# Feed-forward blocks in groups of four, by seven block products in place of eight, with weight sums formed by adding transfers

## Chip, cores and metric

The kernel runs on one NeuronCore of a Trainium2 chip. The metric is the device time of one execution in microseconds (us): here the median of three runs. All tensors are float32.

## What is computed

One inference step of a backbone of two layers. Each layer has a mixer part (attention, pooling, projections) and a feed-forward part (FFN). There are 640 tokens, 128 of context and 512 latent ones, and the model is 1024 wide. The change touches only the FFN and what lies around it:

```
def conv_ffn(h, w_up, conv_w, conv_b, w_down):
    u = h @ w_up
    g, val = u[..., :D_FF], u[..., D_FF:]
    gp = jnp.pad(g, ((0, 0), (1, 1), (0, 0)))
    g = gp[:, :-2] * conv_w[0] + gp[:, 1:-1] * conv_w[1] + gp[:, 2:] * conv_w[2] + conv_b
    return (jax.nn.silu(g) * val) @ w_down
```

`D_FF` is 2816, so `w_up` is 1024 x 5632 and `w_down` 2816 x 1024. The layer then adds the result to the residual `x`, with a gain that the modulation (adaLN) gives.

## The kernel before

Features lie on the 128 partitions and tokens on the free axis. So the normed input of the FFN is 8 tiles (`KT` = 8) of 128 features x 640 tokens, and a half of the tokens (`HT`) is 320 columns. The 2816 inner features are 22 blocks (`NF`) of 128.

**A product.** A float32 matmul is done as three products of reduced parts. `split` makes a high part by a copy on ScalarE (ACT, L251) and a low part by a subtraction on VectorE (DVE, L252). `dense` (L270) then multiplies high by high, high by low, and low by high. One block of weights (128 output features, 1024 inputs) by 640 tokens takes 8 x 3 x 2 = 48 matmuls of 128 x 320, which accumulate in one PSUM tile `mm`.

**Weights.** `load` brings a block of 512 KB by a transfer on SyncE's queue (SP) into one of three `ws` buffers, and `weights` splits it in two operations of 1024 columns into `wh` and `wl` (two buffers each).

**The FFN.** `ffn` goes through the 22 blocks in chunks of 9, 8 and 5 (`CHUNKS`). For a block f it computes the gate block (column block f of `w_up`) and then the value block (column block 22 + f). ScalarE copies the gate into `gp`, VectorE does the convolution (L1148, L1150, L1151), ScalarE a tanh (L1152), VectorE the rest of the silu (L1153, L1154) and the product with the value block (L1159). The result is split into two `u` tiles, which stay in SBUF (20 buffers). At a chunk's end eight output blocks of `w_down` are computed from these `u` tiles, and `residual` (L580) adds each to `x`. The last chunk goes through `project`, which does all output blocks for the first half of the tokens and then for the second, so that the norm's sums can follow.

**Order.** The order of a Tile program is that of its generators. In the first layer, `along` spreads the modulation's products (`ada`: 56 loads of 512 KB, matmuls marked L524) among those of the FFN. The Tile scheduler may move instructions of an engine within its dependencies.

## Time and profile before

| | |
|---|---|
| median of three runs (lowest, highest) | 2315.22 us (2312.96 to 2317.17) |
| span of the profiled execution | 2318.4 us |
| TensorE busy | 2256.9 us (97%) |
| VectorE busy | 1246.9 us (54%) |
| ScalarE busy | 830.5 us (36%) |
| POOL (GpSimd) busy | 150.9 us (7%) |
| DMA, mean over the span | 97 GB/s |

The profiled execution is one more run, and its own time is its span: 3.2 us over the median. A busy share is an average over stages with different limits. What a change in one stage is worth has to be read from that stage: from the chain of waits there and from the windows' busy times.

### The profile page before, as it was taken

The numbers are of one execution on the slowest core, as the hardware profiler recorded it, in microseconds if no ns is written. First come the engines' busy times: TensorE is split into PE (matmuls) and PEld (weight loads), VectorE is DVE, ScalarE is ACT, GpSimd is POOL, SyncE is SP. The second block draws the span as 40 slices with busy tenths as digits, with TensorE's granted clock in tenths as the row PEclk, the third lists the DMA queues.
The fourth block names the chain that finished last, engine by engine and source line by source line (L and its number), as shares of the span: only waits on it lengthen the run. The fifth ranks groups of instructions, "written<-read, shape, count | busy, mean of one in ns | idle before, by whom it ended". The sixth has DMA issues, their size and how long they took to land.

```text
span 2318.4 us, 38736 instructions
## 1 busy us (share of the span) xinstructions
PE 2256.9 (97%) x15863; PEld 2118.1 (91%) x15863; DVE 1246.9 (54%) x2262; ACT 830.5 (36%) x1578; POOL 150.9 (7%) x365
## 2 busy tenths in 40 slices
PE   7999999999999999999999999999999999999998
PEld 4898999998988888999988989999998999999997
DVE  5676736652555432543577767376535654354353
ACT  4466325541423211221334663255423332132132
POOL 1122001210000000000001220021100000000000
PEclk8999999999999999999999999999999999999999
DMA  8242343126505665322142423321124022222221
GB/s 306 69 104 53 99 117 92 46 57 194 177 12 182 189 181 172 98 78 73 55 127 69 104 52 98 82 57 52 46 80 149 23 78 82 73 73 74 74 66 62
DMA packets 283249, 224.69 MB, mean 97 GB/s; under 512 B 12223, under 2 KB 256694, under 8 KB 283072
## 3 DMA queue, kind: packets, MB, share of 16 engines
q1 hardware_dynamic: 282400, 221.43, 33.4%
q8 instruction: 125, 2.05, 0.4%
q0 software_dynamic: 672, 0.79, 0.1%
q14 instruction: 52, 0.43, 0.1%
HBM read 195.54 MB, written 8.29 MB: 88 GB/s over the span
## 4 chain that ended last, share of the span: by engine, by line
PE 81%; DVE 6%; ACT 4%; DMA 3%; issue 2%; POOL 0%; DVEq 0%; ACTq 0%
PE mm L270 50%; PE mm L287 8%; PE d L270 8%; PE o L728 3%; PE pt L637 3%; PE sm L524 2%; PE s L270 1%; DMA ws<-in_w_out 1%; ACT wh L251 1%; PE sm L335 1%; PE s L1012 1%; PE s L1013 1%; PE s L1014 1%; PE s L832 1%; DVE wl L252 1%
## 5 line engine op out<-in xcount | busy, mean ns | idle before, releaser
L252 DVE TENSOR_TENSOR wl<-ws,wh 128x1024 fp32r<-128x1024 f32 (+3 forms) x276 | 277.2, 1009 | 483.5 <-ACT wh L251 469.4
L251 ACT ACTIVATE wh<-ws 128x1024 fp32r<-128x1024 f32 (+3 forms) x276 | 242.8, 886 | 801.6 <-PE mm L270 556.0
L270 PE MATMUL mm<-hh,wh 128*128 128x320 f32 (+1 forms) x2016 | 466.6, 312 | 4.5 <-ACT wh L251 1.5
L270 PE MATMUL mm<-hh,wl 128*128 128x320 f32 (+1 forms) x2016 | 462.0, 310 | 0.8 <-DVE wl L252 0.7
L270 PE MATMUL mm<-hl,wh 128*128 128x320 f32 (+1 forms) x2016 | 461.1, 310 | 0.0
L270 PEld LDWEIGHTS mm<-hh,wh 128*128 128x128 f32 (+1 forms) x2016 | 333.8, 187 | 28.5 <-issue 21.5
L270 PEld LDWEIGHTS mm<-hh,wl 128*128 128x128 f32 (+1 forms) x2016 | 335.4, 187 | 4.6 <-DVE wl L252 1.9
L270 PEld LDWEIGHTS mm<-hl,wh 128*128 128x128 f32 (+1 forms) x2016 | 335.5, 187 | 2.2 <-issue 1.0
L270 PE MATMUL mm<-u,wh 128*128 128x320 f32 x1024 | 193.1, 310 | 0.0
L270 PEld LDWEIGHTS mm<-u,wh 128*128 128x128 f32 x1024 | 160.1, 188 | 6.2 <-issue 6.2
L626 POOL TENSOR_SCALAR p<-p,st 128x640 f32<-128x640 f32 (+1 forms) x160 | 117.8, 737 | 612.6 <-DVE st L625 556.9
L642 DVE TENSOR_TENSOR ptl<-pt,pth 128x512 fp32r<-128x512 f32 (+1 forms) x208 | 118.4, 584 | 46.2 <-PE o L728 23.2
L624 ACT ACTIVATE p<-s,st 128x640 f32<-128x640 f32 (+1 forms) x160 | 113.4, 709 | 67.0 <-DVE st L623 61.5
L641 ACT ACTIVATE pth<-pt 128x512 fp32r<-128x512 f32 (+1 forms) x208 | 103.8, 514 | 66.5 <-PE pt L637 64.7
L623 DVE TENSOR_REDUCE st<-s 128x1 f32<-128x640 f32 (+1 forms) x160 | 113.8, 711 | 21.7 <-PE s L1014 9.2
L580 DVE SCALAR_TENSOR_TENSOR x<-mm,g2h,x 128x128 f32<-128x128 f32 (+2 forms) x144 | 55.9, 434 | 128.2 <-PE mm L270 99.3
L287 PE MATMUL mm<-hh,wr 128*128 128x320 f32 x512 | 118.3, 313 | 3.2 <-ACT hh L251 3.2
L270 PE MATMUL d<-hh,wh 128*128 128x320 f32 x352 | 118.4, 336 | 2.3 <-ACT wh L251 0.5
L270 PE MATMUL mm<-u,wl 128*128 128x320 f32 x512 | 116.5, 308 | 0.0
L637 PE MATMUL pt<-ident,p 128*128 128x128 f32 x672 | 110.1, 276 | 5.7 <-DVE ptl L642 4.4
L270 PE MATMUL d<-hh,wl 128*128 128x320 f32 x352 | 109.5, 311 | 0.0
L270 PE MATMUL d<-hl,wh 128*128 128x320 f32 x352 | 109.3, 310 | 0.0
(312 smaller groups left out, 3954.2 us busy)
## 6 DMA issues: line engine op xcount, KB each, us to landing
wa<-in_w_ada SPq DMA_DIRECT2D x96, 512.0 KB, 3.9
ws<-in_w_up SPq DMA_DIRECT2D x88, 512.0 KB, 3.9
ws<-in_w_in SPq DMA_DIRECT2D x74, 512.0 KB, 4.0
ws<-in_w_down SPq DMA_DIRECT2D x34, 512.0 KB, 4.2
ws<-in_w_out SPq DMA_DIRECT2D x16, 512.0 KB, 4.2
xd<-x SPq DMA_DIRECT2D x16, 320.0 KB, 4.5
x<-xd SPq DMA_DIRECT2D x16, 320.0 KB, 6.5
ws<-in_w_down SPq DMA_DIRECT2D x16, 320.0 KB, 3.2
```

The lines of the kernel that those rows point to most:

```text
L251: nc.scalar.activation(hi, src, AF.Copy)
L252: nc.vector.tensor_tensor(lo, src, hi.bitcast(F32), ALU.subtract)
L270: nc.tensor.matmul(dst, lhsT, r[:, HT * h:HT * h + HT], start=first, stop=last)
L287: nc.tensor.matmul(ps, lhsT, r[:, HT * h:HT * h + HT], start=first, stop=last)
L580: self.nc.vector.scalar_tensor_tensor(self.x[j][:, xs], ps[pi], gate[:, j, s:s + 1], self.x[j][:, xs], ALU.mult, ALU.add)
L623: nc.vector.tensor_reduce(st[:, 0:1], s, axis=AX.XY if len(s.shape) == 3 else AX.X, op=ALU.max, negate=True)
L624: nc.scalar.activation(self.half(p) if len(s.shape) == 3 else p, s, AF.Exp, bias=st[:, 0:1], accum_out=st[:, 1:2])
L626: nc.gpsimd.tensor_scalar(p, p, st[:, 2:3], 1.0, ALU.mult, ALU.mult)
L637: nc.tensor.transpose(pt[:, P * t:P * t + P], p, self.ident)
L641: nc.scalar.activation(hi, v, AF.Copy)
L642: nc.vector.tensor_tensor(lo, v, hi.bitcast(F32), ALU.subtract)
L728: nc.tensor.matmul(state["o"][:, 256 * u:256 * u + 256], vl[a](t + 1), hl[r][:, t, :], start=t == 0 and r == 0, stop=t == 4 and r == 1)
```

## The change

The first two gate and value blocks of a layer, and the last six blocks of the down product, stay as they were. All else is done in **jobs**, 28 in a layer. A job takes two weight blocks side by side, cuts their inputs in two halves and the tokens in two halves, and computes the 2 x 2 blocks of the result by seven block products (Winograd's form of Strassen's scheme) instead of eight. A block product is 12 matmuls (4 input tiles x 3 parts) of 128 x 320, called a slot here, so a job has 84 in place of 96. There are 20 up jobs (gates and values of two blocks each) and 8 down jobs (`CHUNKS` is 8, 8, 6 now).

The seven products need sums and differences:

- **Of weights.** Three of the seven weight operands are sums ("3", "2", "4"). They are formed by transfers that add to their target, on POOL's queue (`fast_sum`): one of 512 KB from `w` in DRAM into a `ws` tile that two plain loads filled before, and two of 256 KB from SBUF to SBUF in a `wb` tile.
- **Of activations.** VectorE forms four mixed blocks ("1" to "4") with `mix_b`, and both parts of each are kept in tiles `tq`. For the up jobs this is done once a layer. For the down jobs, `u` goes to DRAM (`ud`), comes back in groups of eight tiles `ul`, and is mixed and split when the columns change (`chunk`).
- **Of results.** ScalarE copies three of the products out of PSUM (tile `cp`), and VectorE adds.

Splits of weights come as seven of 512 columns a job in place of two of 1024 a block. The convolution's first step moves from VectorE to ScalarE. A job begins every seven slots, and neighbours overlap: `SLOTS` says where each product stands, and `PREP_AT` (in slots from the job's start) when its loads, sums and splits are issued. PSUM holds six banks `q` and two `sm` in this phase. ScalarE, VectorE, POOL and SP keep the program's order while jobs run (`Ordered`). `x` is put into DRAM ahead of the jobs and comes back ahead of the first down job. The last `project` loads and splits its weights a second time for the second half of the tokens, and the modulation's weights have two buffers `wa` of their own.

```diff
-CHUNKS = (9, 8, 5)
+PLAIN_F = 2
+CHUNKS = (8, 8, 6)
...
+        def call(*a, **k):
+            r = f(*a, **k)
+            if self.kern.ordered:
+                self.kern.tc.keep_in_program_order(r)
+            return r
...
+    def fast_load(self, job, what):
+        dma = self.nc.sync.dma_start
+        top, low = job["src"]()
...
+        if what == "sums":
+            dma(parts[:, 0], rows(top)[:, 0])
+            dma(parts[:, 1], rows(low)[:, 0])
...
+        elif what == "top":
+            dma(w.rearrange("p (k n) -> p k n", n=P), top)
...
+            self.flush()
+        else:
+            w = w[:, 0:512].rearrange("p (k n) -> p k n", n=P)
+            dma(w, rows(low)[:, 1])
+            job["a"]["22"] = w
...
+    def fast_sum(self, job, n):
+        a = job["a"]
+        d, x = {"3": (job.get("sums"), job["src"]()[1]), "2": (a.get("2"), a.get("1")), "4": (a.get("4"), a.get("2"))}[n]
+        self.nc.gpsimd.dma_start(d, x, accum_op=ALU.add)
...
+        for t, n, p in at:
+            job = jobs[n]
+            due((n, WSIDE[p]), (job["vn"], VSIDE[p]))
+            first, last = p in ("1", "2", "5"), p != "5"
+            if first:
+                job[bank[p]] = self.q()[:, :HT]
+            ps, w, v = job[bank[p]], job["w"][WSIDE[p]], job["v"][VSIDE[p]]
+            nk = v.shape[2]
+            for k in range(nk):
+                ks = slice(P * k, P * k + P)
+                for i, (x, y) in enumerate(((0, 0), (0, 1), (1, 0))):
+                    nc.tensor.matmul(
+                        ps, w[:, x, ks], v[:, y, k, :], start=first and k == 0 and i == 0,
+                        stop=k == nk - 1 and i == 2, skip_group_check=True)
+                step(t, k)
+                yield 408
+            done(job, p)
...
-                nc.vector.tensor_scalar(
-                    y, gp[:, 0:641], cw[:, 0, f:f + 1], self.conv_b[l][:, f:f + 1], ALU.mult, ALU.add)
...
+            lambda: nc.scalar.activation(
+                y, gp[:, 0:641], AF.Identity, bias=self.conv_b[l][:, f:f + 1], scale=cw[:, 0, f:f + 1]),
...
+            return [(None, lambda f=f: load(f)) for f in range(f0, f0 + 8)], {
+                "1": spl("11"), "2": spl("21"), "5": mix("1") + mix("3") + spl("1") + mix("2") + mix("4") + spl("2"),
+                "7": spl("3"), "4": spl("4"), "3": spl("22")}
...
+        for f0 in (0, 8):
+            loads, works = chunk(f0)
+            behind(jobs[-1], "1", loads)
+            for n in ("1", "2", "5", "7", "4", "3"):
+                behind(jobs[-1], n, works[n])
...
+SLOTS = {"1": 0, "2": 1, "6": 3, "5": 4, "7": 6, "4": 9, "3": 12}
+PREP_AT = {
+    "load": {"sums": -11, "top": -9, "22": -7}, "s3": -9.5, "s2": -5.5, "s4": -4.5,
+    "11": -6, "12": -5, "22": -4, "2": -0.75, "1": -0.25, "3": 0.75, "4": 3.5}
```

**Where instructions stand.** On TensorE, among the last up blocks of the second layer, the order before has three kinds of matmul a tile (`hh`, `hl` the input's parts, `wh`, `wl` the weights'), eight times over, and then the next tile:

```order
L270 MATMUL mm_3011_21267<-hh_66,wh_3009_21263 128x320 x2
L270 MATMUL mm_3011_21267<-hl_67,wh_3009_21263 128x320 x2
L270 MATMUL mm_3011_21267<-hh_66,wl_3010_21264 128x320 x2
L270 MATMUL mm_3019_21332<-hh_66,wh_3017_21328 128x320 x2
L270 MATMUL mm_3019_21332<-hl_67,wh_3017_21328 128x320 x2
L270 MATMUL mm_3019_21332<-hh_66,wl_3018_21329 128x320 x2
```

At that place it now has seven slots: parts of two neighbouring jobs in turn (`hq00`, `hq10`, `hq11` are blocks of the input, `tq` the mixed ones, `wh`, `wl`, `wp` and `hq01` the operands of the weights):

```order
L1363 MATMUL q_2969_19749<-tq_2928_19349,wl_2971_19764 128x320 x12
L1363 MATMUL q_2984_19851<-hq00_66,wh_2974_19773 128x320 x12
L1363 MATMUL q_2988_19871<-hq10_68,wl_2975_19791 128x320 x12
L1363 MATMUL q_2969_19749<-tq_2929_19350,hq01_67 128x320 x12
L1363 MATMUL q_2984_19851<-tq_2927_19348,wp_2981_19836 128x320 x12
L1363 MATMUL q_2998_19935<-tq_2926_19347,wh_2982_19845 128x320 x12
L1363 MATMUL q_2978_19811<-hq11_69,wp_2979_19815 128x320 x12
```

A tile `mm` was finished in one go; now a bank `q` gets 12 matmuls, is left, and gets 12 more some slots later.

On VectorE, where the second layer turns from up to down columns, each down block had one split of its weights and three pieces of the residual's addition:

```order
L252 TENSOR_TENSOR wl_2894_20023<-ws_2892_20020,wh_2893_20022 128x1024
L580 SCALAR_TENSOR_TENSOR x_2661_17996<-mm_2887_19898,g2h1_179,x_2661_17996 128x128
L580 SCALAR_TENSOR_TENSOR x_2661_17996<-mm_2887_19898,g2h1_179,x_2661_17996 128x192
L580 SCALAR_TENSOR_TENSOR x_2661_17996<-mm_2887_19898,g2h1_179,x_2661_17996 128x320
L252 TENSOR_TENSOR wl_2898_20087<-ws_2896_20084,wh_2897_20086 128x1024
L580 SCALAR_TENSOR_TENSOR x_2662_17997<-mm_2891_19962,g2h1_179,x_2662_17997 128x128
L580 SCALAR_TENSOR_TENSOR x_2662_17997<-mm_2891_19962,g2h1_179,x_2662_17997 128x192
```

In the changed order the first such turn (first layer) has the mixing of the loaded blocks `ul` and their splits into `tq`, among the splits of weights (`wp`) and the last blocks' convolution (`u2`, `gp`):

```order
L171 TENSOR_TENSOR ul_1620_10714<-ul_1621_10716,ul_1620_10714 128x320
L171 TENSOR_TENSOR ul_1622_10725<-ul_1623_10727,ul_1622_10725 128x320
L171 TENSOR_TENSOR ul_1627_10741<-ul_1628_10743,ul_1627_10741 128x320
L171 SCALAR_TENSOR_TENSOR u2_1631_10758<-u2_1631_10758,y_1632_10759 128x128
L171 TENSOR_TENSOR gp_1166_7302<-cp_1608_10628,q_1609_10630 128x320
L171 TENSOR_TENSOR ul_1629_10752<-ul_1630_10754,ul_1629_10752 128x320
L171 TENSOR_TENSOR tq_1162_7298<-ul_1620_10714,tq_1162_7298 128x320
L171 TENSOR_TENSOR wp_1640_10850<-wb_1610_10648,wp_1640_10850 128x512
L171 TENSOR_TENSOR tq_1162_7298<-ul_1622_10725,tq_1162_7298 128x320
L171 SCALAR_TENSOR_TENSOR u2_1631_10758<-u2_1631_10758,y_1632_10759 128x512
L171 TENSOR_TENSOR tq_1162_7298<-ul_1627_10741,tq_1162_7298 128x320
L171 TENSOR_TENSOR tq_1162_7298<-ul_1629_10752,tq_1162_7298 128x320
```

These rows are 12 of the 47 operations that stand there from the first split of the new block "11" to the last of the block "2".

On POOL, late in the second layer, stood only the clearing of the padding columns of `gp`, and then the last norm's diagonal matrices:

```order
L1141 MEMSET gp_3060_21916 128x1 x3
L1141 MEMSET gp_3074_22047 128x1 x3
L1141 MEMSET gp_3088_22178 128x1 x3
L1141 MEMSET gp_3102_22309 128x1 x3
L1141 MEMSET gp_3116_22440 128x1 x3
L1231 TENSOR_SCALAR gdiag_3175_22820<-ident_74,colsB_425 128x128 x4
```

Now the adding transfers of each job stand there in a row, with the semaphores that each waits for (DMAHW: loads on SP's queue; DMASW: transfers of POOL's own queue; DVE: a split that has read the target):

```order
L171 DMA ws_3084_20618<-in_w_up 128x8x128 [waits DMAHW7_49,DMAHW6_49]
L171 DMA wb_3088_20652<-ws_3084_20618 128x512 [waits DMASW7_49,DMAHW0_49,DMASW3_49,DVE_49]
L171 DMA wb_3088_20652<-wb_3088_20652 128x512 [waits DMASW0_49,DVE_49]
L171 DMA ws_3103_20755<-in_w_up 128x8x128 [waits DMAHW4_49,DMAHW3_49]
L171 DMA wb_3107_20789<-ws_3103_20755 128x512 [waits DMASW6_49,DMAHW5_49,DMASW2_49,DVE_49]
L171 DMA wb_3107_20789<-wb_3107_20789 128x512 [waits DMASW3_49,DVE_49]
```

The first transfer of a job waits for its two loads, the second for the first transfer among others, the third for the second.

## Rows read from the trace of the kernel before

**Rows 1.** Head of the page: span, busy time by engine, granted clock
```profile
span 2318.4 us, 38736 instructions
...
PE 2256.9 (97%) x15863; PEld 2118.1 (91%) x15863; DVE 1246.9 (54%) x2262; ACT 830.5 (36%) x1578; POOL 150.9 (7%) x365
...
PEclk8999999999999999999999999999999999999999
```

**Rows 2.** The page's chain that ended last, by engine (part 4)
```profile
PE 81%; DVE 6%; ACT 4%; DMA 3%; issue 2%; POOL 0%; DVEq 0%; ACTq 0%
```

**Rows 3.** Pieces of the chain: start us, us, engine, tile, line, count
```profile
716.71 3.71 PE mm L270 x24
...
720.99 4.59 PE mm L270 x30
...
933.33 216.68 PE mm L270 x1476
...
1846.66 401.54 PE mm L270 x2736
```

**Rows 4.** Windows: us, busy of PE, PEld, DVE, ACT, POOL; clock, DMA, GB/s
```profile
10.00:20.00 10.00, 9.04 (x56) 6.43 (x56) 5.01 (x19) 5.97 (x22) 5.02 (x10) 1.00 1.04 391
...
712.00:798.00 86.00, 86.00 (x643) 74.60 (x641) 43.12 (x62) 23.17 (x37) 1.06 (x18) 1.00 0.62 183
...
1846.00:2256.00 410.00, 409.26 (x2787) 408.73 (x2788) 191.61 (x263) 109.76 (x171) 3.38 (x60) 1.00 0.25 74
```

**Rows 5.** DVE's groups, 1846 to 2256 us: busy, mean ns, idle before
```profile
L252 DVE TENSOR_TENSOR wl<-ws,wh 128x1024 fp32r<-128x1024 f32 x57 | 69.8, 1224 | 145.6 <-ACT wh L251 145.1
...
L1150 DVE SCALAR_TENSOR_TENSOR y<-gp,colsD,y 128x641 f32<-128x641 f32 x22 | 19.4, 887 | 0.7
...
L252 DVE TENSOR_TENSOR w<-ws,w 128x512 fp32r<-128x512 f32 x2 | 1.3, 690 | 0.0
...
L1159 DVE TENSOR_TENSOR u<-u,mm 128x320 f32<-128x320 f32 x2 | 1.0, 484 | 0.1
...
L1154 DVE SCALAR_TENSOR_TENSOR u<-fth,y 128x512 f32<-128x512 f32 x22 | 15.1, 685 | 0.0
...
L1153 DVE SCALAR_TENSOR_TENSOR u<-fth,y 128x128 f32<-128x128 f32 x22 | 6.4, 291 | 16.2 <-ACT fth L1152 16.2
```

**Rows 6.** ACT's groups by form, the same stretch
```profile
L1152 ACT ACTIVATE fth<-y 128x641 f32<-128x641 f32 x22 | 16.3, 742 | 62.7 <-DVE y L1151 62.7
...
L1146 ACT ACTIVATE gp<-mm 128x320 f32<-128x320 f32 x22 | 9.7, 443 | 0.0
...
L251 ACT ACTIVATE w<-ws 128x512 fp32r<-128x512 f32 x2 | 1.1, 616 | 0.0
```

**Rows 7.** Timeline of DVE, two instructions of 1950.8 to 1956 us
```profile
1953.40 1.23 DVE L252 TENSOR_TENSOR wl<-ws,wh 128x1024 fp32r<-128x1024 f32 x1
1954.54 0.82 DVE L252 TENSOR_TENSOR u<-u,u 128x640 fp32r<-128x640 f32 x1
```

**Rows 8.** DMA issues: count, KB each, us to landing; one queue
```profile
q0 software_dynamic: 672, 0.79, 0.1%
...
ws<-in_w_up SPq DMA_DIRECT2D x88, 512.0 KB, 3.9
...
ws<-in_w_down SPq DMA_DIRECT2D x16, 320.0 KB, 3.2
...
cos<-in_k_cosm SPq DMA_DIRECT2D x2, 256.0 KB, 3.0
...
sel<-in_k_selb POOLq DMA_DIRECT2D x1, 448.0 KB, 6.9
...
itr<-in_cache_gqa_v SPq DMA_DIRECT2D x2, 64.0 KB, 1.8
```

**Rows 9.** Timeline of POOL at the start: start us, us
```profile
2.52 0.56 POOL L393 DMA_DIRECT2D sel<-in_k_selb  x1
...
4.08 0.50 POOL L410 DMA_DIRECT2D rows<-in_g_norm_ffn  x1
```

More of the change, by code (lines that the diff above doesn't have):

```diff
@@ L33 @@
 NF = DFF // P
-CHUNKS = (9, 8, 5)
+PLAIN_F = 2
+CHUNKS = (8, 8, 6)
+GW = 644
 WINDOWS = (2, 4, 8, 16)
@@ L123, in __getitem__, with __init__ @@
         return self.tiles[at[1]][:, at[2]]
+class Halves:
+    def __init__(self, parts):
+        self.parts = parts
+    def __getitem__(self, at):
+        rows, sl = at
+        h = sl.start // HT
+        return self.parts[h][rows, sl.start - HT * h:sl.stop - HT * h]
 class Feed:
@@ L1124, in out_proj @@
     def out_proj(self, l, m, after):
-        mh = [self.split(a, out=b) for a, b in zip(m, self.h)]
+        for a, (hi, lo) in zip(m, self.h):
+            for h in range(2):
+                sl = slice(HT * h, HT * h + HT)
+                self.split(a[:, sl], out=(hi[:, sl], lo[:, sl]))
+        mh = self.h
         put = lambda j: [self.ph.tile([P, D], F32R, tag="wr", bufs=16, name=self.nm("wr")) for _ in range(2)]
@@ new lines, in ffn, with shifted @@
+        v = {"11": self.hq[0][0], "21": self.hq[1][0], "22": self.hq[1][1], "1": tq[0], "2": tq[1], "3": tq[2],
+             "4": tq[3]}
+        spare = self.hq[0][1].rearrange("p v k n -> p (v k n)")
+        self.w22 = [spare[:, 1024 * a:1024 * a + 1024].rearrange("p (v n) -> p v n", v=2) for a in range(2)]
+        self.n22 = 0
+        us = {}
+        def shifted(h):
+            return [(xs, pi, slice(xs.start + 1 + s, xs.stop + 1 + s)) for s, xs, pi in self.pieces(h)]
+        gps = [self.g(643, name="gp") for _ in range(NGP)]
@@ new lines, in value_plain, with ev @@
+        def value_plain(f):
+            def ev(ps, h):
+                for hh in range(2) if h is None else (h,):
+                    a = self.half(us[f][:, :T], hh)
+                    nc.vector.tensor_tensor(a, a, ps[hh] if h is None else ps, ALU.mult)
+                if h != 0:
+                    out(f)
+            return ev
+        wpt = lambda: self.ph.tile([P, 1024], F32R, tag="wp", bufs=NWP, name=self.nm("wp"))
+        w0 = self.weights(wup(DFF), KT, P, out=(wpt(), wpt()))
+        ws = [self.weights(wup(0), KT, P), self.weights(wup(P), KT, P)]
@@ new lines, in behind @@
+        def behind(job, n, works):
+            after = job.setdefault("after", {})
+            after[n] = after.get(n, []) + works
+        for f0 in (0, 8):
[3 more added lines that the diff above has]
+                behind(jobs[-1], n, works[n])
+            for j in range(0, KT, 2):
+                jobs.append({
+                    "src": lambda f0=f0, j=j: down_src(f0, j), "v": v, "vn": f0, "mixed": True,
+                    "ev": Later(lambda j=j: down_job(j))})
+            if f0 == 0:
+                behind(jobs[-KT // 2], "1", [("x", self.unspill)])
@@ new lines, in ffn, with last_load, last_split @@
+        f0, nf = sum(CHUNKS[:2]), CHUNKS[2]
+        acts, ul = [], {}
+        def last_load(i):
+            self.flush()
+            ul[i] = self.g(name="ul")
+            nc.sync.dma_start(ul[i], ud[f0 + i])
+        def last_split(i, slot):
+            hi, lo = [Halves([slot[:, i % 2, 2 * w + h, :] for h in range(2)]) for w in range(2)]
+            for h in range(2):
+                hs = slice(HT * h, HT * h + HT)
+                self.split(ul[i][:, hs], out=(hi[:, hs], lo[:, hs]))
+            acts.append((hi, lo))
@@ new lines, in ffn @@
+        behind(jobs[-2], "6", [(None, lambda i=i: last_load(i)) for i in range(nf)])
+        for i, (product, name) in enumerate((("6", "2"), ("5", "1"), ("7", "3"))):
+            behind(jobs[-1], product, [(None, lambda n=n, name=name: last_split(n, v[name])) for n in (2 * i, 2 * i + 1)])
+        self.ordered = True
+        yield from self.fast(jobs)
+        self.ordered = False
+        src = lambda j: self.wsrc("w_down", l, P * f0, nf, P * j, P)
+        yield from self.project(src, nf, acts, self.g2h[l], after, None, stat)
```

386 lines of the change are left out of this document (307 added, 79 removed).

## Prediction

> **What bounds the kernel now.** I read the head of the page first. TensorE is busy for 2256.9 of 2318.4 us, VectorE for 1246.9 and ScalarE for 830.5, and the granted clock is at its upper level (2.4 GHz, shown as 9 or 1.00) in every slice but the first [rows 1, 4]. The chain that ended last runs through TensorE for 81% of the span [rows 2]. Within the two feed-forward layers the chain of waits shows more: it holds whole pieces of TensorE with no wait in them. One has 1476 matmuls of 320 columns in 216.68 us, another 2736 in 401.54 us [rows 3]. Both give 0.1468 us a matmul (216.68/1476, 401.54/2736). So in this stage a matmul less is 0.147 us less, as long as nothing else becomes late. The table of windows says how far the others are from that: in 1846 to 2256 us VectorE is busy for 191.6 of 410 us, ScalarE for 109.8, POOL for 3.4, and the DMA engines for 25% of their time [rows 4].
>
> **Matmuls removed (A).** The order has 12676 matmuls of 128x320 before and 12004 after; all others keep their number. That is 672 less: 28 jobs in each of 2 layers, 12 less in each. 672 x 0.1468 = **-98.6 us**. A job is now 84 x 0.1468 = 12.3 us of TensorE (14.1 before), one of its seven slots of 12 matmuls 1.76 us. Everything below is set against 12.3 us a job.
>
> **VectorE and ScalarE in a steady job.** On VectorE one operation starts about 0.09 us ahead of its forerunner's end (1.23 us shown, next start 1.14 later [rows 7]), so I take mean less 0.09: 0.60 for 512 columns, 0.40 for 320, 0.80 for 641 [rows 5]. A job on a gate block has 7 subtractions of 512 (4.2), two convolutions of 2 x 0.80 + 0.20 + 0.60 (4.8) and four or so additions of half blocks (1.3): 10.3 us. A value job has 4.2 + 7 x 0.40 = 7.0, a down job some 7.7. ScalarE in a gate job has 7 x 0.62 + 3 x 0.47 + 0.6 for the halves, and 4 x 0.74 for the convolutions' first steps and tanh [rows 6]: 9.3 us. All lie below 12.3 and beside it: **0**. The cover is thin for gate jobs alone, and a value job follows each.
>
> **The adding chain on POOL (G).** Three transfers of a job follow each other there, and the queue is in order: the 512 KB sum from DRAM (waits for its two loads), the first SBUF sum (waits for that one and for a split), the second (waits for the first); then the next job's. So a job's pace is at least the time to landing of the 512 KB sum, plus that of a 256 KB sum, plus an issue. No adding transfer is in the trace. Bounds: as plain transfers 3.9 us for 512 KB, 3.0 for 256 KB, 0.55 for an issue [rows 8, 9]: 7.5 us. With all doubled, 14.4 us, which is 2.0 over the job: 56 x 2.0 = +113. I take the middle: 64 KB land in 1.8 us and 512 KB in 3.9 [rows 8], so some 2 us do not grow with size, and only what does is doubled by reading the target too: 6.3 + 4.2 + 0.55 = 11.1 us, **0**, with 1.3 us a job to spare. The only row of a large transfer on POOL's queue, 448 KB in 6.9 us, was in the first microseconds, where the DMA share was at its full [rows 4, 8]; it is nearer to the middle than to either end.
>
> The Trainium skill ("DMA: Bandwidth & Descriptors", Anatomy of one DMA, SWDGE path) gives about 2.0 us and bytes over 436 GB/s: 3.2 and 2.6 us, a chain of 6.4 us as an estimate, and the sum would be the same. Of the additions it says nothing there; "Collectives: The Full Stack" says that a reducing transfer reads two sources and so runs at about half the rate of a copy. No row here shows that.
>
> **Chunk changes (B).** Twice in a layer the jobs turn from up to down columns, or to the next eight, and VectorE and ScalarE must then mix and split the eight `u` blocks anew. By the order, VectorE has 47 operations between the first split of the new "11" and the last of "2" at the first change (35 of 320 columns at 0.40, 5 of 512 and one of 512 with three operands at 0.60, 4 of 641 at 0.80, 2 of 128 at 0.21: 21.2 us), 44 at the second (18.4 us). The matmuls that want them come 9.75 slots after the slot in which the loads are issued: 17.2 us, less 3.2 for the first load of 320 KB [rows 8] = 14.0 us. TensorE waits 7.2 + 4.4 us a layer: **+23 us** for two. Low bound 10 (only the excess over the whole 17.2 us, 4.0 + 1.2 a layer), high bound 36 (the splits of other products go on the path too).
>
> **Start of the jobs (C).** The first job's sums can't be prepared long ahead. Load 3.9 + 6.3 + 4.2 + a split of 1.3 = 15.7 us, against two plain blocks of 96 matmuls' time (14.1 us) ahead of it: 1.6 us late in a layer. Its splits also stand behind the two convolutions of the plain blocks in the order, so I take 3 a layer, **+6**; 0 to 20 (nothing, or 10 a layer where the loads start only with the last plain block).
>
> **DMA where adaLN weights come along (D).** In layer 0 56 loads of 512 KB go beside the feed-forward. Behind each of them TensorE has 24 or 30 matmuls (25.5 in the mean), a cycle of 4.28 us for 24, which is 0.76 more than 24 x 0.1468 [rows 3]. A job of 84 takes 3.3 of them, so 56 loads last for 17 jobs of 12.3 + 3.3 x 0.76 = 14.8 us. The stretch with these loads had the DMA engines at 62% for 183 GB/s, the undisturbed one at 25% for 74 GB/s: about 295 GB/s at full share; the first microseconds moved 391 [rows 4]. By 295 a job's 1.7 MB of ada and 1.3 MB of plain loads take 0.39 and 0.30 of its time, the 512 KB sum 0.12 (0.25 if it counts double); by 391 the two others 0.09 (0.18) and `u` 0.06: 0.96 to 1.18 in all. At the low end nothing is lost, at the high one 17 x 14.8 x 0.18 = 45 us; I take a third or so, **+16**. In layer 1 the same sum without ada, over 12.3 us, is 0.70 to 0.94: 0.
>
> **Order as written (E).** Four engines now keep the program's order, so a late operation holds those behind it; the rows cannot show it. 0 to 20 us, **+6** (0.1 us a job). The last projection (F) loads and splits its weights twice: 18 matmuls, 2.6 us, against a split of 768 columns, about 0.9 on either engine [rows 5, 6]: 0.
>
> **Sum.** -98.6 + 23 + 6 + 16 + 6 = -47.6 on the profiled execution's 2318.4 gives 2270.8 us. That span is 3.2 us above the median of 2315.2, so against the median **2268 us**. Its own range, from the bounds of B to E (most of them cannot end alike): 2240 to 2297.
>
> **The rivals.**
> *Stalls absorbed (A alone, nearly).* B at its low bound, C, D and E near 0 to 4: 2315.2 - 98.6 + 13 = 2230 us. For it: TensorE's chain has hundreds of microseconds without a wait [rows 3], and over half of VectorE's time is idle [rows 4]. Against it: by the order VectorE gets some 680 operations more, in bursts at the chunk changes.
> *DMA full in layer 0.* Adds count double and contention is paid: D at 45: 2315.2 - 98.6 + 23 + 6 + 45 + 6 = 2297 us. For it: 62% before the change [rows 4]. Against it: in the first microseconds 391 GB/s were moved [rows 4].
> *The adding chain sets the pace (the other side).* POOL's order is strict, so if its three steps take c us, each job takes c. At 14.4 us: 2315.2 - 98.6 + 113 + 23 + 6 = 2359 us. From c = 13.6 on, the gain is gone (56 x 1.24 = 69.6 = 98.6 - 29). For it: the 448 KB row of 6.9 us [rows 8], and 1024 pieces of 512 bytes in a queue that has carried 672 packets in the whole run [rows 8]. Against it: issues on POOL take 0.50 to 0.56 us whatever they carry [rows 9].
> A rule of the Trainium skill speaks for this rival: by "SBUF - State Buffer", the "DVE blocks DMA" trap, VectorE operations with one input that use both of its ports keep GpSimd from writing descriptors (620 ns become some 3100). VectorE's operations among these jobs have two inputs each, which that page has disturbing GpSimd's reads alone, so I give it 0.02 of this rival's chance; no row here shows it. By its figures, as an estimate, each of three issues would come 2.5 us later and a job's chain would be 18.6 us.
>
> **How the numbers follow.** Chances: the forecast 0.46, stalls absorbed 0.18, DMA full 0.13, adding chain 0.23. The range: 2222 (below the absorbed case, 2216.6 being A without any loss) to 2340, which leaves out the upper half of the chain's case. 0.2% of the time, 4.6 us, is what a measurement here can tell from no change. Faster: 0.46 + 0.18 + 0.13, less 0.06 for their upper ends, and 0.03 for a chain just over the job's time: 0.74; the same 0.05; slower 0.21.
>
> **What the profile after would show.** Right: 14503 matmuls ordered, those of the jobs at 0.147 us, TensorE's pieces without a wait several jobs long, and gaps at two places a layer, ended by VectorE's `tq` splits. The adding transfers of 512 KB land in 5 to 7 us, those of 256 KB in 3.5 to 5. Wrong if each job ends on a wait for a weight sum (`wp`, `wh` split late, released by POOL's queue), if the sums land in more than 8 us, if a job of layer 1 takes much over 12.3 us, or if the granted clock falls to its lower level in the new gaps.

## Result and the profile after

The changed kernel takes 2441.92 us (2432.15 to 2450.62, four runs) against 2315.75 us before: 1.0539 times as long, 95% interval 1.0508 to 1.0569. The forecast was 2268 us, with a range of 2222 to 2340; it was wrong in sign and by 174 us.

The head of its page (span; busy time by engine; granted clock; the chain that ended last, by engine), beside [rows 1, 2]:

```profile
span 2437.1 us, 39673 instructions
...
PE 2225.1 (91%) x15191; PEld 2067.4 (85%) x15191; DVE 1491.6 (61%) x2974; ACT 1064.9 (44%) x2170; POOL 345.8 (14%) x425
...
PEclk8999999999998999998999999999999899998899
...
PE 37%; DMA 15%; DVE 8%; ACT 4%; issue 3%; SPq 1%; POOL 0%; DVEq 0%; ACTq 0%; POOLq 0%
```

The shares of the chain are not to be compared as they stand: it can be followed back only to 759 us here, and to 88 us before, so they add up to 68% and 96% of the span. Of what was followed, TensorE has 54% where it had 84%, and transfers 22% where they had 3%. In five slices besides the first, all where the jobs run, the granted clock is below its upper level.

The windows (columns as in [rows 4]) of 200 us of up jobs in the first layer, of 220 us of steady up jobs in the second, and of all jobs of the second layer:

```profile
780.00:980.00 200.00, 168.71 (x1166) 144.84 (x1164) 99.79 (x185) 72.41 (x136) 35.66 (x32) 0.93 0.97 242
1957.00:2177.00 220.00, 205.12 (x1317) 203.28 (x1318) 144.25 (x264) 106.16 (x209) 53.43 (x50) 0.95 0.93 192
1922.00:2365.00 443.00, 384.34 (x2397) 375.96 (x2398) 292.28 (x572) 201.51 (x413) 101.36 (x88) 0.92 0.90 189
```

The DMA engines are 90 to 97% busy, where they were 25% and, with the adaLN loads, 62% [rows 4]. They move 192 GB/s at a share of 0.93: some 206 GB/s at full share, against 295 before. So it is not bytes alone; the bytes are dearer. The DMA issues (count, KB each, us to landing) and the queue of the adding transfers say which:

```profile
q0 software_dynamic: 87328, 59.53, 18.2%
...
wa<-in_w_ada SPq DMA_DIRECT2D x96, 512.0 KB, 6.4
...
ws<-in_w_up SPq DMA_DIRECT2D x120, 256.0 KB, 5.7
...
ws<-in_w_up POOLq DMA_DIRECT2D x40, 512.0 KB, 7.9
wb<-ws POOLq DMA_DIRECT2D x56, 256.0 KB, 4.8
wb<-wb POOLq DMA_DIRECT2D x56, 256.0 KB, 4.4
```

The 512 KB sum from DRAM lands in 7.9 us (I took 6.3), the SBUF sums in 4.8 and 4.4 (I took 4.2). The plain loads have become slow too: a 512 KB `wa` load lands in 6.4 us in the median, where 512 KB took 3.9 [rows 8]. On POOL's timeline a pair of jobs looks like this (start us, us; in brackets the idle time ahead and its releaser):

```profile
2025.36 0.85 POOL L171 DMA_DIRECT2D wb<-wb  x1 [4.84 <-DMA wb<-ws]
2026.21 1.58 POOL L171 DMA_DIRECT2D ws<-in_w_up  x1
2033.26 0.89 POOL L171 DMA_DIRECT2D wb<-ws  x1 [5.46 <-DVE u L171]
2037.62 0.84 POOL L171 DMA_DIRECT2D wb<-wb  x1 [3.47 <-DMA wb<-ws]
2038.15 1.90 POOL L171 DMA_DIRECT2D ws<-in_w_up  x1
2047.82 0.88 POOL L171 DMA_DIRECT2D wb<-ws  x1 [7.76 <-DMA ws<-in_w_up]
```

From one DRAM sum (`ws<-in_w_up`) to the next it is 11.9 us, and from that to the one at 2054.32 another 16.2; over the 16 jobs from 1957.28 to 2176.87 the mean is 13.7. TensorE needs 12.3 a job. The waits of all engines, and those of TensorE (us in total, times, the longest):

```profile
ACT wp L171 <- DMA wb<-ws: 232.4, 47, 15.9
POOL wb L171 <- DMA wb<-ws: 223.4, 46, 10.7
```

```profile
PE q L1363 <- ACT cp L171: 56.3, 20, 9.1
PE sm L584 <- DMA wa<-in_w_ada: 44.3, 28, 5.0
PE q L1363 <- ACT wh L171: 39.4, 11, 5.1
```

ScalarE waits for an SBUF sum 47 times. Behind that split of `wp` stand, in the written order, the splits of `wh` and the copies `cp`, and these are what TensorE waits for, with the adaLN loads.

From the first matmul of the jobs to the last it takes, in us (28 jobs a layer need 28 x 12.33 = 345 of TensorE alone, and in the first layer 56 x 0.76 = 43 more for adaLN, 388):

| run | median us | before, beside it | ratio, 95% interval | jobs, layer 0 | jobs, layer 1 |
|---|---|---|---|---|---|
| changed kernel | 2441.9 | 2315.8 | 1.0508 to 1.0569 | 495.5 | 443.1 |
| no_sums | 2297.2 | 2318.7 | 0.9877 to 0.9921 | 415.4 | 377.0 |
| plain_copies | 2355.5 | 2318.7 | 1.0143 to 1.0192 | 462.8 | 391.8 |
| early_dram_sum | 2450.6 | 2318.7 | 1.0552 to 1.0586 | 497.3 | 444.3 |
| sums_dve | 2329.4 | 2318.7 | 1.0039 to 1.0069 | 427.6 | 393.3 |
| only_dram_sum | 2334.4 | 2315.3 | 1.0053 to 1.0110 | 434.4 | 387.2 |
| only_sbuf_sums | 2336.6 | 2315.3 | 1.0075 to 1.0105 | 441.2 | 391.8 |
| no_sums_no_turns | 2263.6 | 2315.3 | 0.9760 to 0.9793 | 402.0 | 360.8 |
| sums_pool | 2375.2 | 2315.3 | 1.0244 to 1.0281 | 457.2 | 419.6 |
| dve_early | 2331.8 | 2317.3 | 1.0044 to 1.0080 | 430.4 | 396.6 |
| dve3_dma1_early | 2333.0 | 2317.3 | 1.0045 to 1.0084 | 436.1 | 394.0 |
| dve2_dma2_early | 2351.6 | 2317.3 | 1.0122 to 1.0167 | 449.8 | 394.0 |
| no_top_loads | 2385.4 | 2317.4 | 1.0275 to 1.0310 | 463.8 | 420.4 |
| no_turns_free | 2241.8 | 2317.4 | 0.9659 to 0.9691 | 393.8 | 356.4 |
| dve_dma_at_turns | 2335.7 | 2317.4 | 1.0063 to 1.0093 | 434.0 | 396.9 |
| dve_dma_at_start | 2348.7 | 2317.4 | 1.0124 to 1.0154 | 441.6 | 403.3 |
| sums_dve_free | 2289.2 | 2316.8 | 0.9859 to 0.9889 | 411.7 | 379.6 |
| after_free | 2557.0 | 2316.8 | 1.1010 to 1.1051 | 556.3 | 505.0 |
| dve3_dma1_free | 2284.9 | 2316.8 | 0.9838 to 0.9878 | 413.4 | 376.4 |

### The profile page after: what moved, and what is told of

The parts are those of the page before. It is cut to its first block, busy times and chain, and to the rows that moved or that the text cites. A ratio compares the mean times of both kernels' runs of the same rounds, so it can differ in the third digit from the quotient of the medians.

```text
span 2437.1 us, 39673 instructions
## 1 busy us (share of the span) xinstructions
PE 2225.1 (91%) x15191; PEld 2067.4 (85%) x15191; DVE 1491.6 (61%) x2974; ACT 1064.9 (44%) x2170; POOL 345.8 (14%) x425
## 3 DMA queue, kind: packets, MB, share of 16 engines
q0 software_dynamic: 87328, 59.53, 18.2%
## 4 chain that ended last, share of the span: by engine, by line
PE 37%; DMA 15%; DVE 8%; ACT 4%; issue 3%; SPq 1%; POOL 0%; DVEq 0%; ACTq 0%; POOLq 0%
PE q L1363 11%; PE mm L324 7%; DMA wb<-ws 5%; DMA wa<-in_w_ada 4%; PE q L341 4%; PE d L324 4%; PE mm L341 3%; DMA ws<-in_w_up 2%; DMA ul<-ud 1%; PE o L800 1%; DMA ws<-in_w_down 1%; PE pt L709 1%; SPq L171 1%; PE sm L584 1%; DVE y L171 1%
## 5 line engine op out<-in xcount | busy, mean ns | idle before, releaser
L171 ACT ACTIVATE wh<-ws 128x512 fp32r<-128x512 f32 (+4 forms) x250 | 183.5, 741 | 384.0 <-PE mm L324 206.2
L171 DVE TENSOR_TENSOR wl<-ws,wh 128x1024 fp32r<-128x1024 f32 (+4 forms) x194 | 168.3, 873 | 226.8 <-ACT wh L171 212.0
L324 PE MATMUL mm<-hq,wh 128*128 128x320 f32 (+1 forms) x1472 | 281.0, 311 | 3.2 <-ACT wh L171 1.3
L324 PEld LDWEIGHTS mm<-hq,wh 128*128 128x128 f32 (+1 forms) x1472 | 227.0, 184 | 15.5 <-issue 9.3
L1363 PE MATMUL q<-tq,hq 128*128 128x320 f32 x672 | 133.0, 354 | 52.9 <-ACT cp L171 52.8
L324 PE MATMUL d<-hq,wh 128*128 128x320 f32 x704 | 168.6, 322 | 2.2 <-ACT wh L171 0.5
L324 PE MATMUL mm<-hq,wl 128*128 128x320 f32 (+1 forms) x736 | 169.6, 310 | 0.5 <-DVE wl L171 0.4
L324 PEld LDWEIGHTS mm<-hq,wl 128*128 128x128 f32 (+1 forms) x736 | 120.9, 184 | 4.0 <-issue 1.5
L341 PE MATMUL mm<-hq,wr 128*128 128x320 f32 x768 | 122.0, 312 | 2.1 <-ACT hq L171 2.1
L1363 PE MATMUL q<-tq,wp 128*128 128x320 f32 x672 | 122.9, 332 | 0.3 <-ACT cp L171 0.3
L341 PEld LDWEIGHTS mm<-hq,wr 128*128 128x128 f32 x768 | 113.0, 187 | 10.3 <-issue 7.6
```

The source lines that it names most:

```text
L171: r = f(*a, **k)
L324: nc.tensor.matmul(dst, lhsT, r[:, HT * h:HT * h + HT], start=first, stop=last)
L341: nc.tensor.matmul(ps, lhsT, r[:, HT * h:HT * h + HT], start=first, stop=last)
L1363: nc.tensor.matmul(ps, w[:, x, ks], v[:, y, k, :], start=first and k == 0 and i == 0, stop=k == nk - 1 and i == 2, skip_group_check=True)
```

## Experiments

**Theories.** The profile fits two. By the *chain*, POOL's queue sets the pace: 7.9 + 4.8 + 0.9 for an issue is 13.6 us, nearly the 13.7 seen. By *bandwidth*, the adding transfers use so much of the DMA engines that a job's transfers don't fit in 12.3 us; the long landings are then only how that shows. A third is that the turns between columns and the written order hold TensorE, whatever the sums cost.

The 13.6 us come from medians of the whole run. In the steady jobs themselves, 1957 to 2177 us, the same landings are shorter:

```profile
ws<-in_w_up POOLq DMA_DIRECT2D x17, 512.0 KB, 6.9
...
wb<-ws POOLq DMA_DIRECT2D x16, 256.0 KB, 4.2
```

6.9 + 4.2 + 0.9 is 12.0 us, below the 13.7 and below TensorE's 12.3, so the chain as it is stated does not give the pace there. Of the 16 waits of the first SBUF sum in that stretch, 13 were ended by an operation of VectorE and 3 by the DRAM sum: if waits set the pace, they are longer ones, through the splits on ScalarE and VectorE.

### The sums left out, moved, or made cheap

```diff
 # no_sums: the three adding transfers are left out
+        return
-        self.nc.gpsimd.dma_start(d, x, accum_op=ALU.add)
 # plain_copies
-        self.nc.gpsimd.dma_start(d, x, accum_op=ALU.add)
+        self.nc.gpsimd.dma_start(d, x)
 # early_dram_sum
-    "load": {"sums": -11, "top": -9, "22": -7}, "s3": -9.5, "s2": -5.5, "s4": -4.5,
+    "load": {"sums": -16, "top": -9, "22": -7}, "s3": -13, "s2": -5.5, "s4": -4.5,
```

no_sums. 

> The three adding transfers of every job are left out, so the weight sums are not formed; all else stays, the splits that read the sums included. Theory 1 (the chain of POOL's queue sets a job's pace) and theory 2 (the adding transfers fill the DMA engines) both give the forecast without its chain: 2315 - 98.6 + 23 + 6 + 6 = 2252 us, with jobs of the second layer at 12.3 to 13.1 us and the DMA share there down from 0.92 to some 0.5. Theory 3 (VectorE and ScalarE in written order, and the chunk changes, are what holds TensorE) gives 2400 or more, little below the changed kernel's 2442.

Measured 2297 us: the three adding transfers are worth 145 us. That speaks against the third theory as the main cause, but 2297 is 45 above what the first two gave. Its windows of the second layer, all jobs and 160 us of steady ones, and pieces of its chain:

```profile
1850.00:2227.00 377.00, 363.80 (x2401) 358.07 (x2402) 294.46 (x575) 204.69 (x412) 5.15 (x8) 0.98 0.48 146
1900.00:2060.00 160.00, 160.00 (x1094) 160.00 (x1093) 117.67 (x212) 89.11 (x171) 0.00 (x0) 1.00 0.45 133
```

```profile
1872.82 204.33 PE q L1363 x1392
...
2099.87 6.79 DMA ul<-ud
...
2110.09 2.81 DVE ul L171 x7
...
2130.36 1.21 DVE tq L171 x3
```

1392 matmuls in 204.33 us is 0.1468 each, as before [rows 3]: in steady jobs nothing else holds TensorE, and the DMA engines are at 0.45, 5.5 us a job. What is left shows at the turn: a load `ul` of 6.79 us, and VectorE's mixes and splits.

plain_copies. 

> The same three transfers, in the same places and with the same waits, but they copy and do not add, so the sums are not formed. If adding itself is what is dear (each add reads its target too), the 512 KB one lands in about 5 us in place of 7.9, a 256 KB one in about 3.5 in place of 4.8, POOL's chain falls from 14 to some 10 us, and the time is 2260 to 2300. If a transfer from POOL's queue is dear whatever it does (pieces of 512 bytes, descriptors written by software), landings and time stay as they are, 2420 or more.

Measured 2356 us: neither. The landings fell little, but 86 of the 145 us went. Its queue and issues, and a window of steady jobs in the second layer:

```profile
q0 software_dynamic: 17696, 59.53, 8.0%
...
ws<-in_w_up POOLq DMA_DIRECT2D x40, 512.0 KB, 7.0
wb<-ws POOLq DMA_DIRECT2D x56, 256.0 KB, 3.9
```

```profile
1930.00:2080.00 150.00, 148.91 (x1016) 148.65 (x1015) 112.58 (x204) 84.99 (x163) 25.28 (x38) 1.00 0.72 219
```

The same 59.53 MB take 8.0% of 2362 us as copies, 189 us of all 16 engines, and 18.2% of 2437 us as additions, 444 us: **2.35 times**. (This counts the time of the packets, which can grow where the engines are fuller; the steady jobs further down give 2.2.) They go in 87328 packets in place of 17696, 0.7 KB each and not 3.4. The steady jobs run at TensorE's pace at a DMA share of 0.72, 8.9 us a job. Of the 145 us, then, 86 are for adding and the other 58 or so for three more transfers a job.

early_dram_sum. 

> The 512 KB sum of a job is issued 3.5 slots earlier and its loads 5, so that on POOL's queue it stands ahead of the forerunner's two SBUF sums; the transfers and their bytes are the same. Theory 1 (the queue's chain): the wait for the 512 KB sum (7.9 us to landing) leaves the chain, a job's pace falls from 15.0 us towards 12.3 in the second layer, and the time falls by 56 x 1.5 = 84 us or more, to 2360 or less. Theory 2 (bandwidth): the engines are as full as before, so the time stays within 20 us of 2442.

Measured 2451 us, no gain, as by bandwidth. 220 us of its steady jobs in the second layer:

```profile
1970.00:2190.00 220.00, 202.39 (x1345) 196.91 (x1344) 144.42 (x265) 106.66 (x208) 53.21 (x48) 1.00 0.92 194
```

On its queue the DRAM sum of the next job is under way while the SBUF sums go. It lands in 6.6 us in place of 7.9, but the first SBUF sum now in 7.7 in place of 4.8, and the jobs' pace is 13.8 us (16 from 1970.24 to 2190.77). The chain has other links, and the pace is the same.

sums_dve. The sums are formed by four additions of 512 columns on VectorE, from two plain loads of 512 KB a job; one load and the first additions move by 1.75 and 2.75 slots. (Four of the seven weight operands are sums, not three: the 512 KB transfer of the change forms two of them, "3" and "1", at once.)

```diff
+            dma(w.rearrange("p (k n) -> p k n", n=P), low)
+            job["low"] = parts
...
+        add = self.nc.vector.tensor_tensor
+        if n == "3":
+            add(a["3"], a["2"], job["low"][:, 0], ALU.add)
+            add(a["1"], job["low"][:, 0], job["low"][:, 1], ALU.add)
+        elif n == "2":
+            add(a["2"], a["2"], a["1"], ALU.add)
+        else:
+            add(a["4"], a["4"], a["2"], ALU.add)
```

> The sums are formed by VectorE, four additions of 512 columns a job (2.4 us), from two plain loads of 512 KB; no adding transfers. Theories 1 and 2: some 2250 us as with no sums at all, at most 30 us more where a gate job's VectorE (10.3 + 2.4 = 12.7 us) passes TensorE's 12.3; faster than the kernel before. Theory 3: VectorE's order is the limit, so 2442 or more.

Measured 2329 us: 113 better than the change, 0.5% slower than before, and in neither range (2280 at most by the first two theories, 2442 or more by the third). In 200 us of steady jobs TensorE hardly waits, but VectorE has 185 of 200 us:

```profile
1904.00:2104.00 200.00, 199.43 (x1358) 198.82 (x1358) 185.07 (x336) 106.86 (x213) 0.00 (x0) 1.00 0.37 111
```

### Which sum, and which load

only_dram_sum (`if n == "3":` ahead of the transfer) and only_sbuf_sums (`if n != "3":`). 

> Of the three adding transfers only the 512 KB one from DRAM is left; the two SBUF sums are not formed. By bandwidth (theory 2): a job of the second layer takes 13.0 us of the DMA engines in the changed kernel, 5.6 with no sums; half of the 7.5 us stays, 9.3 us a job, which fits under TensorE's 12.3, so the second layer's jobs come within 10 us of those with no sums (377 us); in the first layer 3.3 ada loads come on top (some 5.5 us, in 14.8), so 14.8 of 14.8: full, and 20 to 50 us are lost there: 2320 to 2350. By the chain (theory 1): 7.9 + 1.9 us, shorter than a job in both layers: 2297 to 2310.

> The 512 KB sum from DRAM is left out (not formed); the two SBUF sums of 256 KB stay. By bandwidth: the same bytes, so about the same as with the DRAM sum alone, 2320 to 2350, and the DMA share in the second layer's jobs at about 0.75. By the chain: 4.8 + 0.9 + 0.9 us a job, far below 12.3: 2297 to 2310.

Measured 2334 and 2337 us, in the ranges that bandwidth gave and above those of the chain. The first fence is the run with the DRAM sum alone, the second that with the SBUF sums alone; each has 200 us of the first layer and 160 of the second:

```profile
780.00:980.00 200.00, 180.88 (x1318) 155.78 (x1317) 113.39 (x208) 82.87 (x156) 18.50 (x12) 0.98 0.86 227
1900.00:2060.00 160.00, 160.00 (x1094) 160.00 (x1093) 120.57 (x220) 89.76 (x170) 20.02 (x14) 1.00 0.80 175
```

```profile
780.00:980.00 200.00, 184.65 (x1333) 158.91 (x1332) 114.98 (x213) 84.40 (x158) 20.37 (x24) 0.97 0.81 231
1900.00:2060.00 160.00, 160.00 (x1093) 160.00 (x1093) 116.81 (x209) 88.80 (x169) 22.78 (x27) 1.00 0.70 174
```

In the second layer both leave TensorE without a gap, at 0.80 and 0.70 of the DMA engines: 9.9 and 8.6 us a job. Less the 5.5 without sums, the DRAM sum takes 4.3 us of all 16 engines and the SBUF sums 3.1. That is 7.4 us where the copies took 3.4 (8.9 - 5.5): 2.2 times. Together it is 12.9 us in 12.3: **they do not fit**, and the changed kernel's 0.93 x 13.7 = 12.7 us agrees. Alone the sums cost 37 and 39 us, together 145.

How soon a transfer lands does not tell how full the engines are. The DRAM sum alone, with the engines at 0.80 and TensorE without a gap, landed later than the 6.9 us of the changed kernel's steady jobs at 0.93:

```profile
ws<-in_w_up POOLq DMA_DIRECT2D x14, 512.0 KB, 9.2
```

no_top_loads: all adding transfers stay, with their order and waits but the one for the load itself; the plain load into the SBUF sums' tile goes from the third job of a layer on.

```diff
+            if old is None:
-            dma(w.rearrange("p (k n) -> p k n", n=P), top)
+                dma(w.rearrange("p (k n) -> p k n", n=P), top)
```

> The changed kernel with all its adding transfers, in the same order and with the same waits on POOL's queue; left out is the plain load of 512 KB into the tile of the two SBUF sums, from the third job of a layer on (the sums go on in the old contents). By bandwidth: a job's 13.0 us of the DMA engines become 11.2, under TensorE's 12.3, so the steady jobs of the second layer go from 13.9 to some 12.4 us and its DMA share stays near 0.9; the layer's jobs take 395 to 415 us in place of 443, the first layer's 440 to 470 in place of 495, and the time is 2340 to 2380. By the chain as such (the order and the waits on POOL's queue, with landings as in the changed kernel): 2420 or more.

Measured 2385 us, with 420 us of jobs in the second layer: 5 us above what bandwidth gave in both figures, and 35 below the chain's. The steady jobs, for which the run was made, do what was expected of bandwidth:

```profile
1950.00:2100.00 150.00, 149.69 (x1016) 149.28 (x1015) 108.51 (x199) 79.46 (x156) 39.89 (x36) 1.00 0.89 175
```

TensorE has 149.7 of 150 us, and the ten jobs from 1972.15 to 2096.00 take 12.4 us each. The same additions on the same queue hold nobody once another transfer is gone. The wait that goes with that load was not it: in the changed kernel's steady jobs it held ScalarE once, for 1.2 us. So in the steady jobs of the second layer the runs speak for bandwidth. It is not the whole: 12.9 us of the engines explain 0.6 us over TensorE's 12.3, and a job took 13.7. The first SBUF sum also lands a little sooner without the load (3.8 us for 4.2), so that longer waits have a part in the rest is not ruled out.

These steady jobs hold only a part of what the sums cost. Counted by 84 matmuls, the 66 us of the second layer (443 against 377 without sums) lie in the first job (7), in the 18 after it (26) and in the last nine, around the turns (33); the 80 us of the first layer lie there with 10, 40 and 31. In the second layer's last nine the engines are at 0.89 in the changed kernel, but either sum alone still costs 9 or 10 us there, and without the plain load only 6 of the 33 come back. No run tells engines and waits apart in these jobs. Nor is 12.9 us a limit at once: four jobs of the first layer, behind the adaLN loads, ran with all sums and without a gap at a share of 0.95.

```profile
1014.00:1063.00 49.00, 49.00 (x336) 49.00 (x336) 35.35 (x65) 26.27 (x51) 13.01 (x12) 1.00 0.95 203
```

A lead of the loads could cover 0.6 us a job for so few jobs; that isn't shown.

### Turns and order

no_sums_no_turns, no_turns_free and sums_pool:

```diff
 # no_sums_no_turns, on no_sums
-            behind(jobs[-1], "1", loads)
-            for n in ("1", "2", "5", "7", "4", "3"):
-                behind(jobs[-1], n, works[n])
 # no_turns_free, on no_sums_no_turns
-        self.ordered = True
+        self.ordered = False
 # sums_pool, on sums_dve
-        add = self.nc.vector.tensor_tensor
+        add = self.nc.gpsimd.tensor_tensor
```

no_sums_no_turns. 

> As with no sums, and besides the loads of the inner blocks, their mixing and their splits at the two turns of a layer are left out (the down jobs multiply old operands). If the turns are what the 65 us are, that TensorE loses in the jobs of the run without sums, 23 us a layer go: some 2250 us. If it is the start of the jobs and the adaLN loads, or operations held by the written order, 2285 or more.

Measured 2264 us: the four turns are worth 34 us without sums.

no_turns_free. 

> As the run without sums and turns, but ScalarE, VectorE, POOL and SP are not held to the program's order among the jobs. If the written order costs what I gave it (term E) or more, the time falls from 2264 us by 6 to 20 us; if the losses left there are the start of the jobs and the adaLN loads, it stays within 5 us or grows.

Measured 2242 us: 22 faster. The written order cost a little more than my upper bound of 20.

sums_pool. 

> As the run with the sums on VectorE, but on GpSimd's own engine (four additions of 512 columns a job). VectorE is 92% busy in the second layer's steady jobs there, with 20 to 30 us lost to it over the run without sums. If GpSimd adds 512 columns in 2 us or less, its 8 us a job hide, and the time is 2297 to 2310, faster than the kernel before; if its operations and VectorE's block one another, it is 2329 or more.

Measured 2375 us, slower. GpSimd's additions took 1446 to 1822 ns, and VectorE slowed down beside them. The same subtraction of 512 columns with the sums on VectorE, then with them on GpSimd, and two of GpSimd's groups (mean ns after the comma):

```profile
L171 DVE TENSOR_TENSOR hq<-ws,hq 128x512 fp32r<-128x512 f32 x12 | 8.2, 687 | 0.0
```

```profile
L171 DVE TENSOR_TENSOR hq<-ws,hq 128x512 fp32r<-128x512 f32 x11 | 19.6, 1779 | 0.0
```

```profile
L171 POOL TENSOR_TENSOR ws<-ws 128x512 f32<-128x512 f32 x10 | 18.2, 1822 | 0.0
L171 POOL TENSOR_TENSOR wb<-wb,ws 128x512 f32<-128x512 f32 x11 | 15.9, 1446 | 13.7 <-DVE wh L171 13.3
```

687 ns against 1779: VectorE is held up beside GpSimd. (Whether GpSimd's additions are slowed by VectorE too no run shows.) The Trainium skill ("SBUF - State Buffer", Who interferes with whom) says that VectorE operations with two SBUF inputs contend with GpSimd operations that read SBUF; this trace agrees, for VectorE's side.

dve_early, dve3_dma1_early and dve2_dma2_early:

```diff
 # dve_early, on sums_dve
-            behind(jobs[-1], "1", loads)
+            behind(jobs[-2], "6", loads)
 # dve3_dma1_early, on dve_early
-            add(a["4"], a["4"], a["2"], ALU.add)
+            self.nc.gpsimd.dma_start(a["4"], a["2"], accum_op=ALU.add)
 # dve2_dma2_early, on dve3_dma1_early
-            add(a["3"], a["2"], job["low"][:, 0], ALU.add)
+            self.nc.gpsimd.dma_start(a["3"], job["low"][:, 0], accum_op=ALU.add)
```

> The run with the sums on VectorE, with the inner blocks' loads at a turn issued four slots earlier. TensorE waited there for a load that landed in 7.4 us and then for VectorE. If the load is the first cause, 4 turns x some 4 us: 2310 to 2318. If VectorE's queue (92% busy) is, 2325 to 2332, as before.

> As the run before it, but the sum that is wanted last in a job (4) is an adding transfer of 256 KB; VectorE forms the other three. By bandwidth: the DMA engines get some 1.6 us a job on 4.5, so they stay far from full in the second layer, and the transfer has some 14 us to land; VectorE gets 0.6 us a job back, 17 us a layer where it sets the pace. 5 to 25 us faster than the run before it. By the chain (an adding transfer costs time wherever it stands): no faster.

> As the run before it, but the second late sum (3) too is an adding transfer of 256 KB, with a plain load of 256 KB more. The DMA engines come to some 8.5 us a job, 0.69 of TensorE's 12.3, and in the first layer with ada to some 12 of 14.8. VectorE gets 1.2 us a job back against the first of these runs. By bandwidth: 5 to 15 us faster than the run before it in the second layer, about the same or slower in the first: 2295 to 2315 in all.

Measured 2332, 2333 and 2352 us: no gain from any of them. The load was not what held a turn. The second late transfer, with its plain load of 256 KB, cost nothing in the second layer (394.0 us both) and 14 us in the first, beside adaLN's loads.

dve_dma_at_turns and dve_dma_at_start (`job["dma"] = n in (20, 21, 24, 25)`, and with 0 and 1). 

> Sums on VectorE, except in the four jobs of a layer whose sums are formed while VectorE mixes and splits the inner blocks (two at each turn), where they are adding transfers as in the change. The DMA engines have room there (0.36 to 0.47 busy with sums on VectorE), and VectorE gets 4 turns x 2 jobs x 2.4 = 19 us back where TensorE waits for it. If so, 2331 less 10 to 19: 2312 to 2321, level with the kernel before. If the landings (some 14 us a job) are later than VectorE's additions, 2330 to 2345.

> As the run before it, with the first two jobs of a layer by adding transfers too, while VectorE mixes and splits the normed input. 2 layers x 2 x 2.4 = 10 us off VectorE where the jobs start, but a chain of some 14 us (two landings) in front of the first job, as in the change: 5 us faster to 15 slower than the run before it.

Measured 2336 and 2349 us: no gain in the first, and 13 us lost in the second. Either VectorE's additions are not what a turn waits for, or the transfers' landings take back what they give; the two runs don't tell which.

sums_dve_free, dve3_dma1_free and after_free (`self.ordered = False` each). 

> Sums on VectorE and no engine held to the program's order among the jobs. By the two runs without sums and turns, the free order is worth 22 us; if that holds with the sums and turns in, 2329 less 22: 2307 us, 0.4% faster than the kernel before. If the order is what keeps VectorE's late work from standing ahead of urgent splits, 2330 or more.

> Three sums on VectorE, the one wanted last by an adding transfer of 256 KB, free order. 2305 to 2312 by the same 22 us; the written order may have held VectorE behind the transfer, and then some 5 us less than the run with all sums on VectorE.

> The changed kernel with free order. The DMA engines stay the limit in the steady jobs (13.0 us of them a job), so it gains at most the 22 us of the order: 2420 to 2442; more than 40 us faster would say that the order, and not the bandwidth, made the adding transfers dear.

Measured 2289, 2285 and 2557 us. **The first two beat both kernels**, the one before by 1.3 and 1.4%; they can't be told from one another. The free order was worth some 40 us with the sums on VectorE. 150 us of steady jobs in the second layer of dve3_dma1_free:

```profile
1900.00:2050.00 150.00, 150.00 (x1026) 150.00 (x1025) 131.96 (x239) 86.25 (x158) 10.12 (x12) 1.00 0.51 135
```

With the adding transfers the free order does the opposite: 115 us slower, where a gain of up to 22 was expected. Its window of 16 steady jobs in the second layer:

```profile
2023.00:2290.00 267.00, 219.30 (x1344) 215.10 (x1344) 144.96 (x264) 107.19 (x208) 53.23 (x48) 0.91 0.77 162
```

A job takes 16.7 us there with the engines at 0.77. So this pace is not set by bandwidth; with these sums waits can set it too. What POOL's sums waited for, first with free order, then in the changed kernel as written:

```profile
POOL wb L171 <- DVE wh L171: 440.6, 45, 15.9
POOL ws L171 <- DMA ws<-in_w_up: 294.0, 33, 127.4
```

```profile
POOL wb L171 <- DVE wh L171: 94.0, 6, 35.1
...
POOL wb L171 <- DVE u L171: 79.2, 14, 10.9
POOL wb L171 <- DVE hq L171: 63.2, 8, 12.3
```

The first SBUF sum may only start when its target has been split. The view names the VectorE operation that ended a wait: mostly `wh` with free order, ten different ones as written. So the sums over all of them have to be compared: 57 waits and 541 us with free order, 48 and 370 us as written. The DRAM sum waited for its plain loads 33 times, 294 us, where it was once and 36 us. Which of the scheduler's moves made splits and loads late wasn't tried.

## Why the prediction was wrong

- **A, -98.6 us: right.** 1392 matmuls of steady jobs at 0.1468 us without a wait, in the run without sums.
- **VectorE and ScalarE hidden: right in the steady jobs without sums.** VectorE has 117.7 of 160 us there, 9.1 us a job (I had 10.3 for a gate job and 7.0 for a value job).
- **D, the DMA engines: the step that failed.** I gave the adding transfers 0.21 to 0.43 of a job of 14.8 us, 3.1 to 6.4 us, and wrote that in the second layer "the same sum without ada, over 12.3 us, is 0.70 to 0.94: 0". Plain loads and `u` were right: 0.45 measured, 0.43 by my figures over 12.3 us. The additions were mis-sized: 7.4 us a job by the windows, 7.9 by the queue's share (444/56). Doubling a copy, my upper end, was too little; 2.2 to 2.35 copies were measured. So the sum passed 1 in both layers. In the second it is 12.9 of 12.3 us. In the first, as an estimate, my 0.75 for adaLN, plain loads and `u` with 7.4/14.8 for the additions is 1.25, which by 14.8 us gives 18.5 us a job; the 14 jobs beside the adaLN loads took 18.6. (The closeness is in part luck: without sums they took 15.8 and not 14.8.) All additions cost 145 us where D and G together had 16, and with that the sign turned. How much of the 145 is bandwidth and how much waits is open in the first jobs and around the turns. The Trainium skill ("Collectives: The Full Stack", The bandwidth ceiling: the fold count and why AG ≠ RS ≠ AR) has a reducing transfer at about half a copy's rate. The factor measured here is larger, and it decides.
- **G, the adding chain: right that it could sum to 13.6 us, wrong as a mechanism.** At that length my own text had the gain gone. But in the steady jobs it sums to 12.0, with the order changed the pace stayed, and with a plain load gone it fell to TensorE's. Issues were not 0.55 us "whatever they carry" but 0.84 to 2.1. By the Trainium skill ("DMA: Bandwidth & Descriptors", Anatomy of one DMA, SWDGE path) the 512 KB one would land in 3.2 us, as an estimate; 7.9 were measured, and 7.0 as a copy. The "DVE blocks DMA" trap of the Trainium skill ("SBUF - State Buffer") played no part that a run shows.
- **B, the turns: +23, measured 34 without sums**, within 10 to 36.
- **E, the written order: +6, bound 20, measured 22** without sums and turns, and 40 with the sums on VectorE. Under the adding transfers the sign turns. I had no row for it and took a tenth of a microsecond a job.
- **C and the rest.** Without sums, turns and written order 25 us are left over 2217 (2241.8 - 2216.6). In the second layer 11 of them lie in the jobs (356.4 - 345), and the trace of no_turns_free has them at the start: the first 84 matmuls take 23.3 us, each later 84 take 12.3 and the last 13.3. I had 3 a layer for C, 10 at most. In the first layer the first 84 matmuls take 26.4 us beside adaLN; how the rest divides is open.
- **The error of 174 us**, with the parts left out in this order, is 129 in the additions (145 - 16), 11 in the turns (34 - 23), 16 in the order (22 - 6) and some 19 in C and what I had not counted; 1 is rounding. In another order the shares would differ: the written order alone is worth 22, 40 or -115 us.
- **The rivals.** The side was that of the adding chain, with 0.23. Its time, 2359, was too low, and its price lay largely in the engines. "DMA full in layer 0" had the mechanism, but only for one layer and at a third of the price.

In the changed kernel the granted clock, too, is lower in the gaps (0.92 over the second layer's jobs, 1.00 in the steady ones without sums). It wasn't tried what that costs by itself; in the run with the early DRAM sum it was 1.00 in steady jobs at the same pace.
